# Sums of G go to DRAM through the buffer of the joined stage's first rows; the last pair's split and store written behind w_down's second products

## The chip, the cores and the metric

One core of one Trainium2 chip runs the whole kernel. The metric is the device time of one execution in microseconds (us), lower being better. Before the change the median of three runs is 1064.61 us (1063.67 to 1065.51).

The names of the engines are TensorE (PE in the profile; its weight loads are PEld), VectorE (DVE), ScalarE (ACT), GpSimd (POOL) and SyncE (SP). SP issues nearly all DMA transfers, in one queue and in order: an issue that waits holds up every issue behind it. GpSimd issues a few transfers of its own.

## The reference, cut to what matters

The kernel computes one decoder layer on 256 tokens of 2048 features, in float32: attention of two kinds, and then a gated feed-forward block. The change lies in the second half of that block.

```python
h = rmsnorm(x, pre_ffn_g[l])
u = causal_dwconv(h @ w_up[l], conv_w[l], conv_b[l])      # 2048 -> 2 x 5632
gate, val = jnp.split(u, 2, axis=-1)
y = (jax.nn.gelu(gate, approximate=True) * val) @ w_down[l]   # 5632 -> 2048
x = x + rmsnorm(y, post_ffn_g[l])
```

G below is gelu(gate) * val, transposed: its 5632 features lie in 44 blocks of 128, and each block holds 256 tokens.

## The kernel before, in words

**Precision.** Each float32 operand is split into a high and a low part. ScalarE casts the high part (`split`, or `w_split` for weights: the lines L120 and L321) and VectorE subtracts it for the low part (L123 and L322). TensorE then makes three products for one: high by high, high by low, low by high. The split weights lie in five rotating buffers (`wpair`), the raw weights in five others (`raw`), and SP refills a raw buffer when VectorE has read it.

**Stages around the change.** The 44 blocks are worked in two halves of 22, and a pair `g` is two blocks, so a half has 11 pairs. In the *gate stage* (about 340 to 578 us) TensorE makes the gate and the value of the pairs 0 to 10 from w_up (L301), ScalarE and VectorE make G of each pair from them. Then come the *w_down products* of the first half for the output columns 0 to 1023 (about 578 to 649 us, L1039). Then the *joined stage* (to about 940 us) makes the second half's gates and values, and between them the first half's products for the columns 1024 to 2047. At the end come the second half's w_down products.

**Seven products in place of eight.** Some pairs multiply a 2 by 2 block matrix of G by one of w_down with seven block products (`seven`). That needs four sums of G's blocks, which GpSimd makes for each pair (`sums_of_y`, L1148 to L1151), and sums of w_down's blocks. The latter are made either on the spot by four VectorE additions (`add`, L1052; pairs 0, 2 and 4 of the columns 0 to 1023), or ahead of time during the gate stage, kept in DRAM (`t_dram`, made by `stage`), and loaded when they are due (pairs 1, 3 and 5). A pair whose sums come from `t_dram` loads them in two pieces: one into a `raw` buffer, the other, `two`, into a buffer of its own with the tag gb0. The other pairs of that part (`four`) are multiplied the plain way.

**Order of the w_down products for the columns 0 to 1023.** The loop runs over i = 0 to 4. At i = 0 it does the first part of pair 0's seven products (banks a, b, e), then 24 plain products, then pair 0's other four (d, f, c, g), and then all seven of pair 1. At i = 1 it does the same with the pairs 2 and 3, at i = 2 with the pairs 4 and 5. Each product of a bank is three matmuls. So TensorE comes to pair 1's t1 and t3 (banks d, f), then to t2 and t4 out of `two` (banks c, g), and then to pair 2.

**Where G's sums go.** The sums of the pairs 0 to 5 stay on the chip. Those of the pairs 6 to 10 are needed only in the joined stage. They are split into a tile `late` of 128 by 1024 (512 KB) with the tag gb0, and GpSimd stores that in DRAM (`s_dram`, L1321 to L1325), from where `late_sums` fetches it when it is due. A tag without a count is one buffer. So `late` of five pairs, then `two` of the pairs 1, 3 and 5, and then the joined stage's rows named `low` take turns in gb0, each waiting for the one before it to be used up. The buffer gb2 holds nothing until the joined stage's first rows, named `top` (512 KB), are loaded into it.

**What orders the work.** TensorE's order is the code's. The other engines' order is set by a scheduler up to the joined stage, which starts an instruction early when its buffers are free; from the joined stage on the order of ScalarE, VectorE and SP is the code's. So an instruction can stand in an engine's queue far from where the code has it.

Of the kernel before, what the change touches and what calls it, by code (L numbers as in the profile page):

```python
# [9 lines left out]
F32R = mybir.dt.float32r  # L10
# [7 lines left out]
P = 128  # L18
# [7 lines left out]
FHALF = 22  # L26
# [9 lines left out]
def hybrid_layer(ctx: ExitStack, tc: tile.TileContext, x, pre_mix_g, w_in, b_forget, sinks,  # L36
# [3 lines left out]
    pe, act, dve, pool, sp = nc.tensor, nc.scalar, nc.vector, nc.gpsimd, nc.sync  # L40
# [13 lines left out]
    def bank(tag="acc"):  # L54
        return ps.tile([P, 512], F32, tag=tag, bufs=4, name="bank_" + tag)
# [13 lines left out]
    UNIT = 1024  # L69
# [250 lines left out]
    def split(hi, lo, src):  # L320
        act.copy(hi, src)  # L321
        dve.tensor_tensor(lo, src, hi.bitcast(F32), op=ALU.subtract)  # L322
# [531 lines left out]
    with tc.tile_pool(name="ffn", bufs=1) as fp:  # L854
# [30 lines left out]
        def rows_of(b):  # L885
            u = ubuf[cnt[0] % NU]
            cnt[0] += 1
            if type(b) is list:
                for m, x in enumerate(b):
                    c = fp.tile([P, 256], F32, tag="cs", bufs=1, name="cs")  # L890
                    act.copy(c, x[:, 256:512])
                    dve.tensor_tensor(u[:, m, 2:258], x[:, 0:256], c, op=ALU.add)
                    pool.tensor_tensor(u[:, m, 2:258], u[:, m, 2:258], rowf, op=ALU.mult)
            else:
                dve.tensor_tensor(u[:, :, 2:258], b.rearrange("p (m c) -> p m c", m=2),  # L895
                                  both(rowf, 256), op=ALU.mult)
            return [u[:, m, :] for m in range(2)]
# [111 lines left out]
        kept_sums = {}  # L1009
# [116 lines left out]
        def gated(us, c0, yy):  # L1126
            gates = []
            for m, u in enumerate(us):
                gates.append(conv(u, c0 // P + m, yy[:, m, :]))
            return gates  # L1130
# [11 lines left out]
        def sums_of_y(half, g, ys):  # L1142
            s = fp.tile([P, 512], F32, tag="s", name="s")
            (a11, a21), (a12, a22) = [(y[:, 0:P], y[:, P:256]) for y in ys]
            s2, s3, s4, s1 = (s[:, i * P:i * P + P] for i in range(4))
            if g < least[half]:
                s1 = a21
            pool.tensor_tensor(s3, a11, a21, op=ALU.subtract)  # L1148
            pool.tensor_tensor(s1, a21, a22, op=ALU.subtract)
            pool.tensor_tensor(s2, s1, a11, op=ALU.subtract)  # L1150
            pool.tensor_tensor(s4, a12, s2, op=ALU.add)  # L1151
            return s
# [5 lines left out]
        def split_sums(half, g, s):  # L1158
            w, *parts = sums_at(half, g)
            split(*parts, s[:, :w])  # L1160

        def joined():

            steps = FHALF // 2
# [58 lines left out]
            for g in range(steps + 1):  # L1223
# [14 lines left out]
                if g:  # L1238
                    if g <= most[1]:
                        s = sums_of_y(1, g - 1, ys)  # L1240
# [49 lines left out]
        for half in range(2):  # L1290
            if half:
                with tc.manual_schedule(engines={mybir.EngineType.Activation, mybir.EngineType.DVE,
                                                 mybir.EngineType.SP}):
                    joined()
            for g in range(0 if half else FHALF // 2):
                c0 = g * 256
                alt = g % 2
                if g == 0:
                    bg = first_gate()
                    order.__exit__(None, None, None)  # L1300
                    bv = [bank(), bank()]
                    proj_T(w_up, DFF + c0, bv, LONG)
                else:
                    bg = bank("att") if alt else bank()
                    proj_S(w_up, c0, bg, LATE if g == 1 else LONG)
                yy = fp.tile([P, 4, 256], F32, tag="yy", bufs=2, name="yy")
                gates = gated(rows_of(bg), c0, yy)
                gelu(gates)
                if g:
                    bv = bank("att") if alt else bank()  # L1310
                    proj_S(w_up, DFF + c0, bv, LONG)
                ys = valued(rows_of(bv), c0, yy, gates)
                if g == 0:
                    for t in range(2):
                        sp.dma_start(x_dram[t * P:(t + 1) * P, :], x_sb[:, t, :])
                s = sums_of_y(0, g, ys)
                for m, y in enumerate(ys):
                    split_G(0, g, m, y)
                if g < most[0]:
                    split_sums(0, g, s)  # L1320
                else:  # L1321
                    x = fp.tile([P, UNIT], F32R, tag="gb0", name="late")
                    split(x[:, 0:512], x[:, 512:1024], s)
                    kept_sums[g] = tc.dram_tile([P, UNIT], F32R, name="s_dram")
                    pool.dma_start(kept_sums[g], x)  # L1325
                if not g:
                    four_of = main.tile([P, 4, 4, 256], F32, tag="y", name="staged")
                    rooms = [four_of[:, i] for i in range(4)]
                    start = 0
                    for at in STORED:  # L1330
                        start = stage(*at, start, 7,
                                      lambda: rooms.append(rooms[0]) or rooms.pop(0))
            if half == 1:
                rest = main.tile([P, KT, 512], F32R, tag="hT", name="rest")
                whole, halves = slice(0, 512), [slice(0, 256), slice(256, 512)]

            assert not todo
            if not half:
                y_sb = main.tile([P, 2, D], F32, tag="y", name="y_sb")
            for n in (0, 2) if half else (0,):  # L1340
                opened = []
                tail = half and n
                at = SEVENS[half][n // 2]
                shared = [bank("att") for _ in range(4 if at else 0)]
                b, e, g = [bank() for _ in range(3)]
                h = None if tail else bank()
                for i in range(FHALF // 2 - len(at)):
                    here = [u for u, x in enumerate(at) if x == i]
                    begun = [lambda u=u: seven(half, n, u, u == len(at) - 1, (b, e, g, *shared), opened)
                             for u in here]  # L1350
                    others = begun[0]() if begun else None
                    four(half, n, len(at) + i, (b, g), opened)
                    if not tail:
                        four(half, n + 1, len(at) + i, (e, h), opened)
                    if others:
                        others()
                    for x in begun[1:]:
                        x()()
                    if at and i == at[-1]:
                        fold(half, n, *shared)  # L1360
                    if i == max((0, *at)):
                        if gains:
                            past = small.tile([P, 1], F32, tag="ry", bufs=2, name="past")
                            tc.keep_in_program_order(
                                pool.tensor_scalar(past, y_sb[:, 1, 1536:1537], 1.0, None,
                                                   op0=ALU.mult))
                        for args, kw in gains:
                            tc.keep_in_program_order(pool.tensor_tensor(*args, **kw))
                    if tail and i == (at[-1] + 4 if at else 0):
                        b1 = [bank("att"), bank("att")]  # L1370
                        for x, cs in zip(b1, halves):
                            pe.matmul(x[:, cs], G[1][0][:, 0:P], G[1][0][:, 0:256], start=True,
                                      stop=False)
                            act.copy(x[:, cs], y_sb[:, 1, 1536:2048][:, cs])
                if half and not tail:
                    gbf = [fp.tile([P, UNIT], F32, tag=f"gb{i}", name=f"gbc_ffn{i}")
                           for i in range(2)]
                    for i, x in enumerate(gbf):
                        cs = slice(i * UNIT, (i + 1) * UNIT)
                        sp.dma_start(x, post_ffn_g[0, cs].partition_broadcast(P))  # L1380
                later_on = None if tail else lambda *args, **kw: gains.append((args, kw))
                for t, x in enumerate((b, g)):
                    down(half, t, n, x, later_on)
                if not tail:
                    for t, x in enumerate((e, h)):
                        down(half, t, n + 1, x, later_on)
# [45 lines left out]
        for t in range(2):  # L1432
            i = sp.dma_start(x_sb[:, t, :], x_dram[t * P:(t + 1) * P, :])
# [58 lines left out]
```

## Time and profile before

| what | value |
|---|---|
| median of three runs | 1064.61 us (1063.67 to 1065.51) |
| the profiled execution, its own time | 1066.2 us |
| its span, first to last instruction | 1064.5 us |
| TensorE busy | 1043.9 us, 98% |
| VectorE busy | 860.3 us, 81% |
| ScalarE busy | 631.7 us, 59% |
| GpSimd busy | 197.8 us, 19% |
| mean granted TensorE clock | 0.992 |
| DRAM traffic | 223 GB/s over the span |

The profile is of one execution. Times in its rows count from the start of the span. A row of the timeline has the start and the length of a group of like instructions, the engine, the line of the code, the operation, what it writes and reads, and the count; in square brackets stands how long the engine had been idle before it, and what it had waited for. A row of the chain of waits has the start, the length and the instruction that held up the end. Rows of stretches give each engine's busy time within a stretch of time, and PEclk, the share of the full clock that TensorE was granted in it. The DMA share is that of 16 engines, and it can go a little over 1.

### The profile page before, as it was taken

How to read it: one execution, taken by the hardware profiler on the slowest of the kernel's cores; microseconds unless marked ns; L12 is line 12 of the kernel's file. 1: busy time of each engine (PE TensorE's matmuls, PEld its weight loads, DVE VectorE, ACT ScalarE, POOL GpSimd, SP SyncE). 2: the span in 40 equal slices, each digit the busy share in tenths (PEclk: the TensorE clock that was granted, in tenths of full speed). 3: DMA queues.
4: the chain of work that ended last, by engine and by line, in shares of the span. 5: the costliest groups of instructions: out<-in, count | busy, mean ns of one | idle time of the engine just before them, and what ended most of it. 6: DMA issues, size and time to landing. Idle time of an engine off the chain costs nothing.

```text
span 1064.5 us, 19057 instructions
## 1 busy us (share of the span) xinstructions
PE 1043.9 (98%) x7225; PEld 958.9 (90%) x7225; DVE 860.3 (81%) x1372; ACT 631.7 (59%) x1041; POOL 197.8 (19%) x244
## 2 busy tenths in 40 slices
PE   9999999999999999999999699999999999999996
PEld 7899988888888999999999489999999999988886
DVE  5999877887468889988888587888888888799793
ACT  6777657667557556546565364555555555656561
POOL 3253255441122311111111200111110000000023
PEclk9999999999999999999999799999999999999999
DMA  8645657555875889999975686666666666767783
GB/s 279 202 128 170 182 158 221 168 169 160 298 235 197 266 265 335 298 317 309 301 240 178 197 248 212 197 199 197 198 199 213 211 214 209 252 196 249 267 311 114
DMA packets 184232, 238.46 MB, mean 224 GB/s; under 512 B 8236, under 2 KB 153036, under 8 KB 183244
## 3 DMA queue, kind: packets, MB, share of 16 engines
q1 hardware_dynamic: 180780, 231.54, 67.6%
q0 software_dynamic: 3040, 5.24, 1.7%
q8 instruction: 56, 0.92, 0.3%
q10 hardware_dynamic: 320, 0.47, 0.1%
q14 instruction: 36, 0.29, 0.1%
HBM read 220.82 MB, written 16.27 MB: 223 GB/s over the span
## 4 chain that ended last, share of the span: by engine, by line
PE 86%; DVE 5%; DMA 3%; ACT 2%; POOL 2%; issue 2%; SPq 0%; DVEq 0%; ACTq 0%; POOLq 0%
PE bank_acc L301 31%; PE bank_acc L1039 13%; PE bank_acc L318 12%; PE bank_att L301 11%; PE bank_att L1039 6%; PE bank_acc L264 5%; PE bank_acc L271 3%; DVE wpair L123 2%; PE bank_att L318 1%; POOL scr L451 1%; PE bank_att L519 1%; DMA raw<-in_w_in_dram 1%; PE bank_att L484 1%; PE bank_att L528 1%; DMA low<-in_w_down_dram 1%
## 5 line engine op out<-in xcount | busy, mean ns | idle before, releaser
L123 DVE TENSOR_TENSOR wpair<-raw,wpair 128x1024 fp32r<-128x1024 f32 (+3 forms) x311 | 372.1, 1221 | 58.9 <-ACT wpair L120 57.8
L120 ACT CAST wpair<-raw 128x1024 fp32r<-128x1024 f32 (+3 forms) x310 | 312.9, 1030 | 125.7 <-PE bank_acc L301 51.5
L301 PEld LDWEIGHTS bank_acc<-hT,wpair 128*128 128x128 f32 x2976 | 341.3, 188 | 1.8
L301 PE MATMUL bank_acc<-hT,wpair 128*128 128x256 f32 x2976 | 342.1, 276 | 0.0
L1039 PE MATMUL bank_acc<-wpair,G 128*128 128x512 f32 x546 | 136.1, 392 | 0.3 <-DVE wpair L322 0.2
L1039 PEld LDWEIGHTS bank_acc<-wpair,G 128*128 128x128 f32 x546 | 102.9, 189 | 22.6 <-DVE wpair L322 0.6
L301 PE MATMUL bank_att<-hT,wpair 128*128 128x256 f32 x1056 | 120.7, 276 | 0.0
L301 PEld LDWEIGHTS bank_att<-hT,wpair 128*128 128x128 f32 x1056 | 120.2, 188 | 0.1
L264 PE MATMUL bank_acc<-hT,wpair 128*128 128x512 f32 x384 | 94.9, 394 | 0.0
L264 PEld LDWEIGHTS bank_acc<-hT,wpair 128*128 128x128 f32 x384 | 69.5, 188 | 13.2
L318 PE MATMUL bank_acc<-wpair,oT 128*128 128x512 f32 x336 | 78.0, 391 | 0.0
L318 PEld LDWEIGHTS bank_acc<-wpair,oT 128*128 128x128 f32 x336 | 62.6, 188 | 12.8
L1148 POOL TENSOR_TENSOR s<-yy 128x128 f32<-128x128 f32 x16 | 13.7, 853 | 309.3 <-DVE yy L1139 309.3
L900 ACT ACTIVATE yy<-u,cw 128x256 f32<-128x256 f32 x88 | 48.3, 594 | 31.7 <-DVE u L895 28.4
L321 ACT CAST wpair<-low 128x1024 fp32r<-128x1024 f32 x32 | 33.7, 1053 | 35.3 <-PE bank_acc L301 14.0
L895 DVE TENSOR_TENSOR u<-bank_acc,rowf 128x512 f32<-128x512 f32 x31 | 21.3, 689 | 38.5 <-PE bank_acc L301 38.5
L321 ACT CAST G<-yy 128x256 fp32r<-128x256 f32 x44 | 16.3, 405 | 58.8 <-DVE yy L1139 36.5
L271 PE MATMUL bank_acc<-hT,wpair 128*128 128x256 f32 x384 | 49.5, 280 | 0.0
L271 PEld LDWEIGHTS bank_acc<-hT,wpair 128*128 128x128 f32 x384 | 47.4, 188 | 1.4
L318 PE MATMUL bank_acc<-wpair,hT 128*128 128x384 f32 (+1 forms) x288 | 47.7, 321 | 0.0
L321 ACT CAST wpair<-raw 128x1024 fp32r<-128x1024 f32 (+1 forms) x39 | 34.4, 896 | 19.6 <-PE bank_acc L1039 6.6
L318 PEld LDWEIGHTS bank_acc<-wpair,hT 128*128 128x128 f32 x288 | 45.4, 188 | 0.1
(270 smaller groups left out, 1378.2 us busy)
## 6 DMA issues: line engine op xcount, KB each, us to landing
raw<-in_w_up_dram SPq DMA_DIRECT2D x176, 512.0 KB, 5.2
raw<-in_w_down_dram SPq DMA_DIRECT2D x53, 512.0 KB, 4.8
raw<-in_w_in_dram SPq DMA_DIRECT2D x51, 512.0 KB, 5.5
raw<-in_w_out_dram SPq DMA_DIRECT2D x32, 512.0 KB, 4.2
staged<-in_w_down_dram SPq DMA_DIRECT2D x36, 256.0 KB, 6.4
t_dram<-staged SPq DMA_DIRECT2D x18, 512.0 KB, 6.6
low<-in_w_down_dram SPq DMA_DIRECT2D x16, 512.0 KB, 4.6
raw<-t_dram SPq DMA_DIRECT2D x13, 512.0 KB, 5.7
```

Of the source, the lines that this page charges most:

```text
L120: i1 = act.copy(hi[:, cs], raw[:, cs])
L123: i2 = dve.tensor_tensor(lo[:, cs], raw[:, cs], hi[:, cs].bitcast(F32), op=ALU.subtract)
L264: pe.matmul(b, hi[:, a, m * P:(m + 1) * P], hT[:, kt, 0:512], start=(kt == 0), stop=(last == (0, kt)))
L271: pe.matmul(b[:, 256:512], lo[:, a, m * P:(m + 1) * P], hT[:, u * 4 + a, 0:256], start=False, stop=(last == (1, u * 4 + a)))
L301: pe.matmul(b[:, m * 256:(m + 1) * 256], ws[:, a, m * P:(m + 1) * P], hT[:, kt, i * 256:(i + 1) * 256], start=not begun, stop=last == (low ...
L318: pe.matmul(b, a, r[:, cols], start=(first and i == 0), stop=(last and i == 2))
L321: act.copy(hi, src)
L451: pool.tensor_tensor(dst, dst, row, op=ALU.mult)
L895: dve.tensor_tensor(u[:, :, 2:258], b.rearrange("p (m c) -> p m c", m=2), both(rowf, 256), op=ALU.mult)
L900: act.activation(y, u[:, 2:258], AF.Identity, bias=cw[:, 3, ch:ch + 1], scale=cw[:, 2, ch:ch + 1])
L1039: pe.matmul(b, x, r, start=b not in opened and not i, stop=closes and i == 2)
L1148: pool.tensor_tensor(s3, a11, a21, op=ALU.subtract)
```

## The change

The split and the store of a pair's sums become a function, `keep_sums`, whose tile `late` has the tag gb2 in place of gb0. The pairs 6 to 9 call it where they did before. The last pair, 10, calls it later in the code: in the loop over the w_down products, at i = 1, behind the products of the pairs 2 and 3.

```diff
+        def keep_sums(g, s):
+            x = fp.tile([P, UNIT], F32R, tag="gb2", name="late")
+            split(x[:, 0:512], x[:, 512:1024], s)
+            kept_sums[g] = tc.dram_tile([P, UNIT], F32R, name="s_dram")
+            pool.dma_start(kept_sums[g], x)
...
                 if g < most[0]:
                     split_sums(0, g, s)
-                else:
-                    x = fp.tile([P, UNIT], F32R, tag="gb0", name="late")
-                    split(x[:, 0:512], x[:, 512:1024], s)
-                    kept_sums[g] = tc.dram_tile([P, UNIT], F32R, name="s_dram")
-                    pool.dma_start(kept_sums[g], x)
+                elif g < FHALF // 2 - 1:
+                    keep_sums(g, s)
...
                     for x in begun[1:]:
                         x()()
+                    if not half and i == 1:
+                        keep_sums(FHALF // 2 - 1, s)
```

No instruction is added or taken away. TensorE, ScalarE and GpSimd have their instructions in the same order as before; on ScalarE and VectorE the last pair's split still stands ahead of the split of pair 1's t1 and t3 (the row `wpair<-raw` before `wpair<-two`), although the code now has it behind. SP's queue and a few rows of VectorE are what moves.

The first place is SP's queue in the gate stage, at about 400 us. Here `staged` and `t_dram` belong to the sums of w_down that are made ahead, and each row has in brackets the semaphores that it waits for: DMAHW those of earlier transfers of SP, DMASW of GpSimd's, the others of engines. Before:

```order
L75 DMA raw<-in_w_up_dram 128x4x256 [waits DMAHW0_49,DVE_49]
L923 DMA staged<-in_w_down_dram 128x2x256 [waits DMAHW1_49]
L923 DMA staged<-in_w_down_dram 128x2x256 [waits DMAHW2_49]
L75 DMA raw<-in_w_up_dram 128x4x256 [waits DMAHW3_49,DVE_49]
L932 DMA t_dram<-staged 512x1x256 [waits DMAHW4_49]
```

And the same place now:

```order
L75 DMA raw<-in_w_up_dram 128x4x256 [waits DMAHW7_49,DVE_49]
L923 DMA staged<-in_w_down_dram 128x2x256 [waits DMAHW0_49]
L923 DMA staged<-in_w_down_dram 128x2x256 [waits DMAHW1_49]
L75 DMA two<-t_dram 128x1024 [waits DMAHW5_49,DMAHW2_49]
L75 DMA raw<-in_w_up_dram 128x4x256 [waits DMAHW3_49,DVE_49]
L932 DMA t_dram<-staged 512x1x256 [waits DMAHW4_49]
```

The load of pair 1's `two` has come here from a place about 190 us later, and waits for the store of its two halves. In exchange a row has gone from SP's queue at the start of the gate stage: the load of the first `top`, issued there at 338.8 us before.

The second place is SP's queue at the w_down products of the pairs 1 to 3, at about 590 to 608 us. Before:

```order
L75 DMA raw<-in_w_down_dram 128x512 [waits DMAHW5_49,DVE_49]
L75 DMA raw<-in_w_down_dram 128x1024 [waits DMAHW7_49,DVE_49]
L75 DMA two<-t_dram 128x1024 [waits DMASW3_49,DMASW2_49,DMASW5_49,DMASW1_49,DMASW0_49]
L75 DMA two<-t_dram 128x1024 [waits DMAHW7_49,DMAHW0_49,DVE_49]
L75 DMA raw<-t_dram 128x1024 [waits DMAHW1_49,DVE_49]
```

And now:

```order
L75 DMA raw<-in_w_down_dram 128x512 [waits DMAHW5_49,DVE_49]
L75 DMA raw<-in_w_down_dram 128x1024 [waits DMAHW7_49,DVE_49]
L75 DMA two<-t_dram 128x1024 [waits DVE_49]
L75 DMA top<-in_w_down_dram 128x1024 [waits DMASW3_49,DMASW5_49,DMASW2_49,DMAHW0_49,DMASW1_49,DMASW0_49]
L75 DMA raw<-t_dram 128x1024 [waits DMAHW1_49,DVE_49]
```

The first of the two rows `two` was pair 1's, and waited for GpSimd's stores of `late`; the one that is left is pair 3's, and waits for VectorE to have read pair 1's. The wait for GpSimd's stores now stands on `top`, one row later, ahead of pair 3's `raw<-t_dram`.

The third place is VectorE at the pairs 1 and 2, from the low part of pair 1's `two` on. The rows L1052 are pair 2's additions, `low` is its second load, and the two rows L123 are the plain products' weights of i = 1. This is a piece of the difference, with - for before and + for now:

```order
 L322 TENSOR_TENSOR wpair<-two,wpair 128x1024
 L322 TENSOR_TENSOR wpair<-raw,wpair 128x512
-L322 TENSOR_TENSOR wpair<-low,wpair 128x1024
 L1052 TENSOR_TENSOR raw<-raw 128x512
-L123 TENSOR_TENSOR wpair<-raw,wpair 128x1024
+L322 TENSOR_TENSOR wpair<-low,wpair 128x1024
 L1052 TENSOR_TENSOR raw<-raw,low 128x512
 L123 TENSOR_TENSOR wpair<-raw,wpair 128x1024
 L1052 TENSOR_TENSOR low<-low,raw 128x512
-L322 TENSOR_TENSOR wpair<-raw,wpair 128x1024
-L1052 TENSOR_TENSOR low<-low 128x512
+L123 TENSOR_TENSOR wpair<-raw,wpair 128x1024
+L1052 TENSOR_TENSOR low<-low 128x512
+L322 TENSOR_TENSOR wpair<-raw,wpair 128x1024
```

Each of the additions has moved one place forward, and so `low` stands behind one addition, and the first of the plain weights behind two. The same piece comes once more, at the pairs 3 and 4.

## The prediction

> **What bounds the kernel now.** I read the page first, of an execution with a span of 1064.5 us. Its row of engines and its row of granted clock say:
>
> ```profile
> PE 1043.9 (98%) x7225; PEld 958.9 (90%) x7225; DVE 860.3 (81%) x1372; ACT 631.7 (59%) x1041; POOL 197.8 (19%) x244
> ...
> PEclk9999999999999999999999799999999999999999
> ```
>
> TensorE is busy for 98% of the span, so only its idle time and its slow time can be won without changing its work. The one slice in which its clock falls short is the 23rd of 40, at about 585 to 612 us. The second view is that of who waited for whom, TensorE alone:
>
> ```profile
> PE bank_att L1039 <- ACT wpair L321: 8.4, 2, 7.6
> ```
>
> It heads that list: 8.4 us in two waits, the longest 7.6, in the w_down products (L1039), for ScalarE's cast of weights. The third view is the chain of waits between 555 and 660 us, which tells what held up that cast:
>
> ```profile
> 591.38 5.41 DMA s_dram<-late
> ...
> 596.87 3.66 DMA two<-t_dram
> ```
>
> To be read downwards: the last pair's split is stored in DRAM (5.41 us); only then is gb0 free, and pair 1's `two` is loaded into it (3.66 us); the cast comes behind. Both transfers lie bare on the path. The fourth view is TensorE's timeline:
>
> ```profile
> 580.14 5.60 PE L1039 MATMUL bank_acc<-wpair,G 128*128 128x512 f32 x24
> 585.58 0.84 PE L1039 MATMUL bank_att<-wpair,G 128*128 128x512 f32 x3
> ...
> 591.35 0.50 PE L1039 MATMUL bank_att<-wpair,G 128*128 128x512 f32 x1 [0.84 <-ACT wpair L321]
> 592.61 0.73 PE L1039 MATMUL bank_att<-wpair,G 128*128 128x512 f32 x2 [0.76 <-DVE wpair L322]
> 593.18 0.99 PE L1039 MATMUL bank_att<-wpair,sums 128*128 128x512 f32 x3
> 601.72 0.79 PE L1039 MATMUL bank_att<-wpair,sums 128*128 128x512 f32 x1 [7.56 <-ACT wpair L321]
> 602.98 1.22 PE L1039 MATMUL bank_att<-wpair,sums 128*128 128x512 f32 x2 [0.47 <-DVE wpair L322]
> 604.00 1.48 PE L1039 MATMUL bank_acc<-wpair,G 128*128 128x512 f32 x3
> 605.28 1.48 PE L1039 MATMUL bank_att<-wpair,G 128*128 128x512 f32 x3
> ...
> 608.34 5.60 PE L1039 MATMUL bank_acc<-wpair,G 128*128 128x512 f32 x24
> ```
>
> From 580.14 to 585.58 it starts 24 matmuls in 5.44 us, 0.227 us each: full pace. From 604.00 to 605.28 three take 1.28 us, 0.427 each: half pace. The stretches of the fifth view say why:
>
> ```profile
> 590.30:593.70 3.40, 1.80 (x7) 1.05 (x6) 1.92 (x2) 0.99 (x2) 0.74 (x2) 1.00 0.84 214
> 593.70:594.20 0.50, 0.47 (x2) 0.00 (x0) 0.00 (x0) 0.00 (x0) 0.00 (x0) 0.54 1.12 301
> 594.20:601.70 7.50, 0.00 (x0) 0.00 (x0) 0.00 (x0) 1.07 (x2) 0.00 (x0) 0.50 0.60 215
> 601.70:607.30 5.60, 5.11 (x11) 3.73 (x12) 5.60 (x7) 3.52 (x5) 0.00 (x0) 0.50 0.30 97
> 607.40:613.00 5.60, 5.60 (x26) 4.63 (x25) 4.41 (x6) 3.17 (x4) 0.12 (x1) 1.00 0.75 232
> ```
>
> The third number from the end is the granted clock: full until 593.7, half until about 607.35, then full. It fell before the long wait, while TensorE still worked, right after the two short gaps at 590.5 and 591.8.
>
> **The stall goes.** Pair 1's `two` is now loaded at about 404 us, ahead of its use by some 190 us. The cast of `two` then follows ScalarE's cast before it. ScalarE's rows:
>
> ```profile
> 589.73 0.62 ACT L321 CAST late<-s 128x512 fp32r<-128x512 f32 x1 [3.83 <-POOL s L1151]
> 590.25 1.04 ACT L321 CAST wpair<-raw 128x1024 fp32r<-128x1024 f32 x1
> 600.63 1.04 ACT L321 CAST wpair<-two 128x1024 fp32r<-128x1024 f32 x1 [9.33 <-DMA two<-t_dram]
> 601.58 0.61 ACT L321 CAST wpair<-raw 128x512 fp32r<-128x512 f32 x1
> ```
>
> Casts of that size follow each other at 0.95 us (600.63 to 601.58), so `two` is cast from 591.20 to 592.24. The weight buffer that it needs is that of pair 0's t1 and t3, last read before TensorE turned to pair 1, ahead of the row of 591.35. Pair 1's f starts at 593.18 and its three matmuls are issued by 593.86. Behind them stand c and g of pair 1 and a, b and e of pair 2: 15 matmuls, 3.40 us at full pace. The 24 plain products could start at 597.26 in place of 608.34. **That is 11.08 us**: 7.86 us of standing still (593.86 to 601.72), and 3.22 us by which 601.72 to 608.34 is longer than 3.40, from half pace and the 0.47 us wait.
>
> **What is late next.** VectorE. Its rows after the stall:
>
> ```profile
> 591.33 1.23 DVE L322 TENSOR_TENSOR wpair<-raw,wpair 128x1024 fp32r<-128x1024 f32 x1 [0.25 <-ACT wpair L321]
> 601.70 1.23 DVE L322 TENSOR_TENSOR wpair<-two,wpair 128x1024 fp32r<-128x1024 f32 x1 [9.15 <-ACT wpair L321]
> 602.85 0.69 DVE L322 TENSOR_TENSOR wpair<-raw,wpair 128x512 fp32r<-128x512 f32 x1
> 603.45 1.22 DVE L322 TENSOR_TENSOR wpair<-low,wpair 128x1024 fp32r<-128x1024 f32 x1
> 604.58 0.69 DVE L1052 TENSOR_TENSOR raw<-raw 128x512 f32<-128x512 f32 x1
> 605.18 1.22 DVE L123 TENSOR_TENSOR wpair<-raw,wpair 128x1024 fp32r<-128x1024 f32 x1
> ```
>
> A large one takes a place of 1.15 us, a small one or an addition 0.60. The row of 591.33 stays, since the last pair's split is still ahead of it; so `two` comes at 592.48, the small one at 593.63, the addition at 594.23, `low` at 594.83, the second addition at 595.96, and the first plain weights (L123) at 596.56, done by 597.79. The two additions that the new order puts ahead cost the plain weights one more place, 0.60 us. The second plain matmul, the first that needs the low part, would start at 597.49: 0.30 us late. Later steps have room: the second plain weights come two places on, at about 599.5, and are needed 2.7 us after the first. At full clock the gain is 11.08 - 0.30 = **10.78 us**.
>
> **The clock, which the trace doesn't show for the changed kernel.** The two short gaps stay, for ScalarE still waits for GpSimd's sums until 589.7. If the clock falls after them as it did, TensorE goes on at half pace from 593.7. One end: it doesn't fall, cost nothing. The other: half pace lasts as long as it did once work had begun again, 601.72 to 607.35, 5.6 us; at 0.427 us that is 13 matmuls where 25 fit, 12 late by 0.227, 2.7 us. There is no reason for a gain. I take the middle, 1.34 us, since the long stretch of before had 7.86 us of idleness ahead of it and a further wait within. This delay covers the 0.30 us of VectorE. **The sum: 11.08 - 1.34 = 9.74 us.** By the Trainium skill (TensorE: Matmul & The Clock Gate, Part 1: The HAM clock gate), full clock comes back after about 3.4 us of sustained work; as an estimate from that page half pace would then cost 1.6 us and the gain be 9.5 us.
>
> **Edits at nothing, and their cover.** Moving the first `top` from 338.8 to about 597 us: its first cast is at 636.4.
>
> ```profile
> L321 ACT CAST wpair<-top x1: 624/624/624, 636.4 to 636.4; 128x512 fp32r<-128x512 f32 x1
> ```
>
> The five stores of `late` took this long from issue to landing:
>
> ```profile
> DMA to landing us min/median/max: 3.3/3.4/5.4
> ```
>
> And loads of the same size from `t_dram`, in the median of 13:
>
> ```profile
> raw<-t_dram SPq DMA_DIRECT2D x13, 512.0 KB, 5.7
> ```
>
> On SP `top` now waits for the last store, due by 596.8, and pair 3's `raw<-t_dram` and all later loads queue behind it. That one waits for the L123 above anyway, 597.8, so the wait is covered by 1.0 us; landing at 603.5, cast and subtracted it is ready by 605.8. TensorE needs it 45 matmuls (10.2 us) after 597.26, at 607.5 or later. If that cover of 1.7 us went, each us more would cost one. Pair 3's `two` goes out at 593.7, nine us earlier than now, and has longer still. The stores of the pairs 6 to 9 change their buffer only. The shift holds to the end: behind 607 us TensorE's waits come to this one of 0.2 us.
>
> ```profile
> PE bank_acc L1039 <- DVE wpair L322: 0.2, 1, 0.2
> ```
>
> The stretch where `two` is put now:
>
> ```profile
> 400.00:412.00 12.00, 12.00 (x108) 12.00 (x107) 11.90 (x22) 6.85 (x9) 1.07 (x2) 1.00 1.03 341
> ```
>
> TensorE is busy throughout, while the DMA engines are full (share 1.03). At 341 GB/s 512 KB take 1.5 us, which the weights loaded ahead should hide: from nothing to 1.5 us, taken as nothing.
>
> **How the numbers follow.** The profiled execution took 1066.2 us, 1.6 more than the median, so the same step would put its like at 1056.5; I take the gain from the median: 1064.61 - 9.74 = 1054.9 us. A measurement of this kernel can tell about 0.2%, 2.1 us, from no change.
>
> - **Forecast**, 1054.9 us: 0.52.
> - **The clock stays full**: the gaps of 0.84 and 0.76 us alone don't bring it down in most executions. For it: what follows them now is work, not idleness. Against it: the 0.54 in the row of 593.7. 1064.61 - 10.78 = 1053.8 us: 0.28. The same page (HAM oscillation) asks for a gap over about 3.4 us before the clock falls, which gives this time; the row of 593.7 doesn't agree.
> - **A new wait at pair 3**, for `raw<-t_dram` behind `top`, or for VectorE: a load of 5.7 us taking twice that costs 5.7 - 1.7, less what half pace hides, about 3.4 us. Against it: the DMA share of 0.30 there. 1058.3 us: 0.08.
> - **The early load hurts the gate stage**, 1.5 us: 1056.4 us: 0.07.
> - **Nothing comes of it**: the wait at 594 is ended by something else just as late. The order of ScalarE, where the written move of the last split changed nothing, shows how that could be; but no other partner of `two` is late. 1064.6 us: 0.03.
> - **Slower**: GpSimd's last store starves beside loads that now go on, and holds SP behind `top`. It starts to cost when it lands after 600.8 (pair 3 needed at 608.8, less 5.7, 1.05 and 1.23) and costs one for one; over 12 us of that, a landing after 612.6, is slower than before by 2.1 us. Five stores took 3.3 to 5.4; this would need 21. At 24 us it gives 1069.5 us: 0.02.
>
> The range goes from the full clock less what the runs of before spread downward (1064.61 - 1063.67 = 0.9), 1052.9, to the new wait at pair 3, 1058.3. Faster: all but the last two, 0.95; same 0.03; slower 0.02.
>
> **What would show it.** Right: the wait of 7.6 us is gone; the cast of `two` starts near 591.2; the plain products of i = 1 start between 597.5 and 599.9; the two short gaps are still there; pair 3 waits for nothing. The granted clock behind 593 tells forecast and first rival apart. Wrong: a wait over 2 us at the pairs 2 or 3, any gap between 400 and 560, or an SP row `top` issued well behind 597.

## The result and the profile after

| | before | after |
|---|---|---|
| median, same chip, in turns | 1065.06 us (1063.67 to 1066.15, 4 runs) | 1054.6 us (1053.86 to 1055.45, 4 runs) |
| the profiled execution, its own time | 1066.2 us | 1055.45 us |
| its span | 1064.5 us | 1053.7 us |
| mean granted TensorE clock | 0.992 | 0.997 |

The ratio is 0.9903, with a 95% interval of 0.9886 to 0.992: about 1% faster. The forecast was 1054.9 us. One execution of the experiments below, the profiled one of `low` behind pair 3's loads, took 1746.65 us at a granted clock of 0.556 and stands in none of the times.

The page's rows of engines and of granted clock, after:

```profile
PE 1041.1 (99%) x7225; PEld 957.0 (91%) x7225; DVE 861.3 (82%) x1372; ACT 631.7 (60%) x1041; POOL 199.3 (19%) x244
...
PEclk9999999999999999999999999999999999999999
```

The digit 7 at the 23rd slice is gone. Who waited for whom, TensorE alone, between 555 and 660 us after (the columns are the total, the count and the longest wait):

```profile
PE bank_att L1039 <- ACT wpair L321: 1.4, 1, 1.4
PE bank_att L1039 <- DVE wpair L322: 0.8, 1, 0.8
```

The wait of 7.6 us is gone, and what is left are the two short gaps ahead of pair 1. ScalarE's timeline after:

```profile
589.19 0.62 ACT L321 CAST late<-s 128x512 fp32r<-128x512 f32 x1 [3.83 <-POOL s L1151]
589.71 1.04 ACT L321 CAST wpair<-raw 128x1024 fp32r<-128x1024 f32 x1
590.66 1.04 ACT L321 CAST wpair<-two 128x1024 fp32r<-128x1024 f32 x1
591.61 0.61 ACT L321 CAST wpair<-raw 128x512 fp32r<-128x512 f32 x1
```

`two` is cast right behind the cast before it, with no idle time in front: the row of before had 9.33 us of it. The first row is the cast of the last pair's sums: ScalarE still waits 3.83 us for GpSimd there, as before, and pair 1's casts come behind it. TensorE's timeline after, with the same matmuls as the rows of before:

```profile
588.60 0.84 PE L1039 MATMUL bank_acc<-wpair,sums 128*128 128x512 f32 x3
590.80 0.51 PE L1039 MATMUL bank_att<-wpair,G 128*128 128x512 f32 x1 [1.36 <-ACT wpair L321]
592.06 0.73 PE L1039 MATMUL bank_att<-wpair,G 128*128 128x512 f32 x2 [0.75 <-DVE wpair L322]
592.64 2.33 PE L1039 MATMUL bank_att<-wpair,sums 128*128 128x512 f32 x6
594.76 1.48 PE L1039 MATMUL bank_acc<-wpair,G 128*128 128x512 f32 x3
596.04 1.09 PE L1039 MATMUL bank_att<-wpair,G 128*128 128x512 f32 x3
596.97 0.85 PE L1039 MATMUL bank_acc<-wpair,G 128*128 128x512 f32 x3
597.65 0.84 PE L1039 MATMUL bank_acc<-wpair,sums 128*128 128x512 f32 x3
598.33 5.60 PE L1039 MATMUL bank_acc<-wpair,G 128*128 128x512 f32 x24
```

From f (592.64) to the 24 plain products (598.33) it takes 5.69 us; before it was 593.18 to 608.34, 15.16 us. So the step itself gives 9.47 us. The three matmuls at 594.76 take 1.28 us up to the next row, which is half pace, and those at 596.97 take 0.68, full pace. The stretches after say the same of the granted clock (third number from the end):

```profile
590.30:593.10 2.80, 1.54 (x6) 1.05 (x7) 2.54 (x4) 2.80 (x5) 0.55 (x1) 1.00 1.00 237
593.20:596.50 3.30, 3.30 (x10) 2.52 (x9) 3.27 (x5) 2.04 (x3) 0.00 (x0) 0.50 1.05 331
596.60:602.00 5.40, 5.40 (x26) 4.45 (x25) 5.34 (x6) 2.98 (x4) 0.00 (x0) 1.00 0.81 278
```

The clock fell after the two gaps, as before, but for 3.4 us (593.14 to 596.55) where before it was 13.65 (593.74 to 607.39). SP's queue after:

```profile
593.17 0.33 SPq L75 DMA_DIRECT2D two<-t_dram  x1
596.65 0.33 SPq L75 DMA_DIRECT2D top<-in_w_down_dram  x1
597.38 0.33 SPq L75 DMA_DIRECT2D raw<-t_dram  x1
```

`top` waits for the last store, and pair 3's `raw<-t_dram` goes out behind it at 597.38 and lands at 603.90. TensorE doesn't wait for it.

### The profile page after: what moved, and what is told of

It reads as the page before. It is cut to its first block, busy times and chain, and to the rows that moved or that the text cites. A ratio compares the mean times of both kernels' runs of the same rounds, so it can differ in the third digit from the quotient of the medians.

```text
span 1053.7 us, 19053 instructions
## 1 busy us (share of the span) xinstructions
PE 1041.1 (99%) x7225; PEld 957.0 (91%) x7225; DVE 861.3 (82%) x1372; ACT 631.7 (60%) x1041; POOL 199.3 (19%) x244
## 4 chain that ended last, share of the span: by engine, by line
PE 84%; DVE 6%; DMA 3%; ACT 2%; issue 2%; POOL 2%; SPq 0%; DVEq 0%; ACTq 0%; POOLq 0%
PE bank_acc L301 31%; PE bank_acc L1039 12%; PE bank_acc L318 12%; PE bank_att L301 10%; PE bank_att L1039 6%; PE bank_acc L264 5%; PE bank_acc L271 3%; DVE wpair L123 2%; PE bank_att L318 1%; DMA low<-in_w_down_dram 1%; POOL scr L451 1%; PE bank_att L519 1%; DMA raw<-in_w_in_dram 1%; PE bank_att L484 1%; PE bank_att L528 1%
## 5 line engine op out<-in xcount | busy, mean ns | idle before, releaser
L123 DVE TENSOR_TENSOR wpair<-raw,wpair 128x1024 fp32r<-128x1024 f32 (+3 forms) x311 | 372.2, 1222 | 58.5 <-ACT wpair L120 57.6
L1039 PE MATMUL bank_acc<-wpair,G 128*128 128x512 f32 x546 | 135.4, 391 | 0.1
L1039 PEld LDWEIGHTS bank_acc<-wpair,G 128*128 128x128 f32 x546 | 102.5, 189 | 21.9 <-DVE wpair L123 0.5
L322 DVE TENSOR_TENSOR wpair<-raw,wpair 128x1024 fp32r<-128x1024 f32 (+1 forms) x39 | 39.6, 1029 | 7.5 <-ACT wpair L321 7.1
```

The source lines that it names most:

```text
L123: i2 = dve.tensor_tensor(lo[:, cs], raw[:, cs], hi[:, cs].bitcast(F32), op=ALU.subtract)
L1039: pe.matmul(b, x, r, start=b not in opened and not i, stop=closes and i == 2)
```

## The experiments

All times are medians on the same chip as a run of the kernel before; each ratio is to that, whose median was 1065.27, 1066.08 and 1066.3 us on the three chips. The theory is that of the prediction: what was won is the row of store, load and cast through gb0, and what is left are two short gaps and a clock that falls after them. The first rival is that the new place of the split in the code does it, and the second question what the two gaps and the clock are worth. Where the expectations use letters, A is the prediction's account, the rivals have the letters behind it, and F is the theory that the place alone led to.

**The buffer alone.** The kernel before with one tag changed; the split and the store stay where the code had them.

```diff
-                    x = fp.tile([P, UNIT], F32R, tag="gb0", name="late")
+                    x = fp.tile([P, UNIT], F32R, tag="gb2", name="late")
```

> One half of the change alone: the sums of all five pairs pass through gb2, and the last pair's split and store stay where the code had them before. Theory A, the buffer does it all and the written place nothing, since the scheduler puts the split back where it was: the time of the changed kernel, 1054.6 us within its spread of about 1 us, with the two short gaps of TensorE at pair 1 and its cast of `two` right behind the cast before it. Rival B, the later place in the code gives a part of the gain: over 1056.5 us, and a wait at pair 1 of over 2 us.

Measured: 1055.7 us (1054.4 to 1059.24), ratio 0.991 (0.9892 to 0.9929). The order of the instructions on every engine is that of the changed kernel. So in this change the buffer makes the gain, and the new place in the code makes nothing, since the scheduler sets the split back ahead of pair 1. The two times differ by 1.1 us, less than the spread of this run. Its profiled execution is its slowest; there the half clock lasted 6.83 us:

```profile
593.30:599.90 6.60, 6.04 (x14) 4.78 (x15) 6.57 (x9) 4.55 (x6) 0.00 (x0) 0.50 1.05 324
```

**The place alone.** The changed kernel with the old buffer. With gb0 the last pair's tile can only come behind pair 3's `two`, so here the split really is late.

```diff
-            x = fp.tile([P, UNIT], F32R, tag="gb2", name="late")
+            x = fp.tile([P, UNIT], F32R, tag="gb0", name="late")
```

> The other half alone: the last pair's split and store stand behind the products of the pairs 2 and 3 in the code, and pass through gb0 as before. Now gb0 is taken by pair 1's and pair 3's `two` first, and the split can't be put back; pair 5's `two` waits for the last store. Theory A says that what costs is a `two` that waits for a store, wherever it stands: pair 1 waits for nothing and the two short gaps go as well (about 2.1 us, and 1.6 us of half pace in those executions where the clock fell), and at pair 5 a wait may come: the last `two` of pair 3 is read at about 603, so the split ends at 606, the store lands at 609.5 to 611.7, `two` at 613 to 618.5, ready 2.3 us later, 615.5 to 621, and TensorE wants it at about 620.6. So 1051.0 to 1052.5 us, at worst 1 us more. Rival B, the place gives only a part and the buffer is needed for the rest: 1056 to 1060 us, with a wait of several us at pair 5.

Measured: 1056.37 us (1056.17 to 1057.13), ratio 0.9912 (0.9899 to 0.9926). That missed, and lies in the range of rival B, but without the wait of several us at pair 5 that it goes by. The stall is gone here too, so the place takes it away as the buffer does, once the split can't be put back. The first half of the expectation came true: no gaps of 1.36 and 0.75 us, a clock that stays full, and at 597 us a lead of 4.0 us over the changed kernel. But it was given back. GpSimd's timeline in this kernel, the four sums of the last pair:

```profile
585.38 5.78 POOL L1148 TENSOR_TENSOR s<-yy 128x128 f32<-128x128 f32 x1 [20.65 <-DVE yy L1139]
591.13 0.90 POOL L1149 TENSOR_TENSOR s<-yy 128x128 f32<-128x128 f32 x1
592.11 1.32 POOL L1150 TENSOR_TENSOR s<-s,yy 128x128 f32<-128x128 f32 x1
593.51 0.79 POOL L1151 TENSOR_TENSOR s<-yy,s 128x128 f32<-128x128 f32 x1
```

In the changed kernel the first of them takes 2.91 us and the other three 0.45 or 0.46 each. VectorE beside them, whose instructions of these sizes take 0.69 and 1.22 us elsewhere:

```profile
590.16 0.68 DVE L322 TENSOR_TENSOR wpair<-raw,wpair 128x512 fp32r<-128x512 f32 x1
590.88 0.83 DVE L1052 TENSOR_TENSOR raw<-raw 128x512 f32<-128x512 f32 x1
591.63 1.48 DVE L322 TENSOR_TENSOR wpair<-low,wpair 128x1024 fp32r<-128x1024 f32 x1
593.04 0.94 DVE L1052 TENSOR_TENSOR raw<-raw,low 128x512 f32<-128x512 f32 x1
```

While GpSimd's first sum runs, and up to the first of these rows, each VectorE instruction starts some 0.08 us before the one ahead of it ends. The first pause is that from 590.84 to 590.88, and GpSimd's first sum ends at 591.16, 0.32 us after its start. The additions and the low parts behind it are the slow ones. And SP, where pair 4's `low` waits for GpSimd to have read the buffer that it shares with `yy`:

```profile
594.32 0.33 SPq L75 DMA_DIRECT2D low<-in_w_down_dram  x1
...
596.51 0.55 SPq L75 DMA_DIRECT2D raw<-t_dram  x1
```

In the changed kernel `low` goes out at 589.18. Here it and what is behind it go out with pair 3's load, which takes 8.4 us to land (604.90). TensorE then waits at pair 3:

```profile
607.36 0.72 PE L1039 MATMUL bank_att<-wpair,G 128*128 128x512 f32 x2 [0.76 <-DVE wpair L322]
...
613.30 5.07 PE L1039 MATMUL bank_acc<-wpair,G 128*128 128x512 f32 x21 [0.68 <-DVE wpair L123]
```

The lead is 2.6 us at 604.7, 1.4 behind the first of these, 0.2 at the second, and at 946 us the kernel is 0.7 behind. From this came a further theory: GpSimd's first sum doesn't come to its end while VectorE runs without a pause, and what is queued behind it (the late split, `low` on SP) gives the gain back.

**The split behind pair 1's.** The changed kernel, buffer gb2, with the split of the last pair tied behind the cast and subtraction of `two`.

```diff
-            split(x[:, 0:512], x[:, 512:1024], s)
+            parts = split(x[:, 0:512], x[:, 512:1024], s)
+            if pair1:
+                for i, first in zip(parts, pair1):
+                    tc.add_manual_dep(
...
```

> The changed kernel, with the last pair's split tied behind the split of pair 1's `two` on ScalarE and VectorE, so that it really stands later. Theory A: the two short gaps (1.4 and 0.8 us) go, and with them the fall of the clock: no granted clock under 1.00 between 20 and 1040 us in the profile, and 2.1 us plus 1.6 us (in about half of the executions) less than the changed kernel: 1051.0 to 1052.5 us. Rival D, the gaps only cover a wait for VectorE, which has the same work to do before the plain products: a wait of 1.5 us or more at pair 2 or at the plain products, and 1053.5 us or more.

Measured: 1057.8 us (1054.87 to 1059.82, 6 runs), ratio 0.9923 (0.9906 to 0.9939). That missed too: the time is rival D's, though no single wait reaches the 1.5 us that it names. GpSimd is late again. Its first sum, and VectorE's rows around its end (line numbers are shifted by up to 3):

```profile
586.11 5.18 POOL L1151 TENSOR_TENSOR s<-yy 128x128 f32<-128x128 f32 x1 [20.54 <-DVE yy L1142]
```

```profile
589.76 1.21 DVE L321 TENSOR_TENSOR wpair<-two,wpair 128x1024 fp32r<-128x1024 f32 x1
593.99 0.69 DVE L321 TENSOR_TENSOR wpair<-raw,wpair 128x512 fp32r<-128x512 f32 x1 [3.02 <-ACT wpair L321]
```

The sum ends at 591.29, 0.32 us after VectorE fell idle at 590.97. ScalarE stood before the late split for 4.19 us meanwhile, and held the casts behind it; the last store went out at 595.83 and landed at 605.26. `top` waits for that store, and the loads behind it on SP go out late:

```profile
605.35 0.33 SPq L75 DMA_DIRECT2D top<-in_w_down_dram  x1
```

```profile
610.66 0.62 ACT L321 CAST wpair<-raw 128x512 fp32r<-128x512 f32 x1 [2.84 <-DMA raw<-in_w_down_dram]
```

TensorE is 0.2 us ahead of the changed kernel at 611 us and 2.3 behind at 614, which is nearly all that it loses. Here the clock stayed full without a gain. In the changed kernel the two engines show the same thing, earlier:

```profile
584.74 2.91 POOL L1148 TENSOR_TENSOR s<-yy 128x128 f32<-128x128 f32 x1 [19.45 <-DVE yy L1139]
```

```profile
586.11 1.23 DVE L322 TENSOR_TENSOR wpair<-raw,wpair 128x1024 fp32r<-128x1024 f32 x1
589.84 0.69 DVE L322 TENSOR_TENSOR late<-s,late 128x512 fp32r<-128x512 f32 x1 [2.50 <-ACT late L321]
```

VectorE falls idle at 587.34 and the sum ends at 587.65, 0.31 later. The same time from VectorE's first pause to the end of the sum is 0.31 to 0.33 us in all nine traces in which GpSimd makes this sum. No run takes VectorE's work away, so that it is what holds the sum rests on these times.

The Trainium skill (SBUF — State Buffer, Who interferes with whom) has a rule for this: a VectorE instruction with two inputs in SBUF contends with a GpSimd instruction that reads SBUF, over a port that one of them holds at a time. The sums that end 0.3 us after the start of VectorE's first pause agree with it.

**The last pair alone.** The kernel before, with gb2 for the last pair only.

```diff
-                    x = fp.tile([P, UNIT], F32R, tag="gb0", name="late")
+                    x = fp.tile([P, UNIT], F32R, name="late",
+                                tag="gb2" if g == FHALF // 2 - 1 else "gb0")
```

> Only the last pair's sums pass through gb2, the other four through gb0 as before, all at the old place in the code. Pair 1's `two` then waits for the store of the pair before the last, landed at 569, and is loaded at about 569 to 577 in place of 403. Theory A, only the last store was in the way and it doesn't matter how early `two` comes: the changed kernel's time, 1054.6 us, at most 1 us more, since `low` of pair 0 is issued behind that load. Rival C, the load had to leave the w_down stage altogether, whose transfers are in each other's way: pair 0 or 1 waits over 1.5 us more, 1056.5 us or more.

Measured: 1056.62 us (1056.11 to 1057.03), ratio 0.9913 (0.99 to 0.9927), within the spread of the buffer alone. By the expectation this is rival C's number, just over its 1056.5 us. But the wait that rival C names isn't there: `two` is loaded from 568.80 to 572.63, and the gap ahead of pair 1 is 1.98 us, as in the profile of the buffer alone, where `two` comes at 403. So for the stall to go it is enough that the last pair's store doesn't stand before `two`; whether the early load is worth a further us the intervals leave open. The clock fell for 3.4 us.

**The sums on VectorE.** The changed kernel, in which VectorE makes the last pair's four sums.

```diff
-            pool.tensor_tensor(s3, a11, a21, op=ALU.subtract)
+            q = dve if not half and g == FHALF // 2 - 1 else pool
+            q.tensor_tensor(s3, a11, a21, op=ALU.subtract)
...
```

> The changed kernel, with the last pair's four sums made by VectorE in place of GpSimd. Theory F, formed after the first runs: TensorE's two short gaps come from GpSimd, whose first sum takes 2.9 us where 0.5 is its usual time, until VectorE pauses; and where the gaps were taken away by other means (the split tied behind, or put behind pair 3) VectorE didn't pause, the sum took 5.2 and 5.8 us, and SP's load of `low` for pair 4, which waits for that sum, held up pair 3's loads. If the sums cost VectorE four short operations of about 0.25 us and nothing waits for GpSimd, the plain products start near 594.6 in place of 598.3, the clock doesn't fall, and the time is 1051.0 to 1053.0 us. Rival D, VectorE is the next bound and gives all of it back: 1053.5 us or more, with waits for VectorE of over 2 us at the pairs 1 to 3.

Measured: 1053.89 us (1052.78 to 1056.05), ratio 0.9884 (0.9869 to 0.99). That is 0.9 us over the range of theory F and in rival D's, though no wait for VectorE comes near its 2 us. TensorE's row of the plain products and the cast of pair 3's load on ScalarE:

```profile
594.51 5.60 PE L1039 MATMUL bank_acc<-wpair,G 128*128 128x512 f32 x24
```

```profile
603.71 1.05 ACT L321 CAST wpair<-raw 128x1024 fp32r<-128x1024 f32 x1 [2.60 <-DMA raw<-t_dram]
```

Both gaps go and the clock stays full: the plain products start 3.82 us earlier than in the changed kernel, as forecast (594.6). But now TensorE is early enough to wait for pair 3's load (0.77 us at 606), and 1.44 us of the lead is left at 946. So the wait for GpSimd's sums is what made the two gaps.

**The gaps filled.** The changed kernel with ten matmuls of no use into bank b, six ahead of pair 1's d and four behind its first matmul. They change bank b's sum, and with it pair 1's part of the output; the expectation is wrong in that they take no part.

```diff
+                    fill(b, 6)
+                    pe.matmul(d, s1[0], t1[0], start=False, stop=False)
+                    fill(b, 4)
```

> The changed kernel, with ten matmuls of zeros added into bank b where TensorE stands still at pair 1: six before the first of t1's products and four between it and the next (0.22 us each). They take no part in the result. If the two gaps are what brings the clock down, there is no stretch under 1.00 between 20 and 1040 us, the 15 matmuls ahead of the plain products take 3.4 to 3.7 us in place of 5.0, and the median is 1053.4 to 1054.2 us with a spread under 1 us. Rival: the clock falls for another reason, or the added matmuls come in the way: 1054.6 us or more, with half pace in some runs.

Measured: 1054.44 us (1054.29 to 1055.37), ratio 0.9889 (0.9874 to 0.9904). The profile has no idle time at pair 1 and a full clock throughout:

```profile
592.99 1.53 PE L1039 MATMUL bank_att<-wpair,sums 128*128 128x512 f32 x6
...
597.28 3.07 PE L1039 MATMUL bank_acc<-wpair,G 128*128 128x512 f32 x11
```

From f to the plain products it takes 4.29 us, against 5.69 with the clock's fall. The 15 matmuls ahead of the plain products take 3.60 us, as expected; the median is 0.2 us over the expected range and 0.2 under the rival's. The time is too near the changed kernel's to show the 1.4 us by itself. Nor does one profile show that the filling kept the clock up, as the next run tells.

**The changed kernel again**, on the chip of the last two.

> The changed kernel once more, as the measure for the other three on the same chip: 1054.6 us, between 1053.8 and 1055.5; those executions in which the clock fell some 1.3 us longer than the others.

Measured: 1054.98 us (1054.43 to 1057.48), ratio 0.9897 (0.9882 to 0.9912); one execution lies 2 us over the expected range. In its profile the same two gaps stand (1.25 and 0.76 us), and the clock did not fall:

```profile
593.20:596.50 3.30, 3.30 (x16) 2.49 (x15) 3.27 (x6) 2.06 (x4) 0.00 (x0) 1.00 0.99 322
```

From f (592.82) to the plain products (597.12) it takes 4.30 us, as with the gaps filled. So the fall is not fixed by the order of the instructions: it came in four of the five profiles that have these gaps (before, after, the buffer alone, the last pair alone).

**`low` behind pair 3's loads.** The place alone, with pair 4's `low` set behind pair 3's loads on SP.

```diff
+                if not half and not n and u == 4:
+                    for first in pair3:
+                        tc.add_manual_dep(
+                            issued[-1].ins, first.ins.name,
...
```

> The place alone again (last pair's split behind pair 3, buffer gb0), with pair 4's `low` tied on SP behind pair 3's loads. Theory F: then the slow GpSimd sum holds up only `low`, which has time; pair 3's `raw<-t_dram` goes out before 596 and lands by 603, TensorE's wait for its cast at 606 to 607 goes, and the time is 1 to 2 us under that of the place alone: 1054.4 to 1055.4 us. Rival: the SP queue was not what came late, and VectorE's waits at the plain products remain: 1056 us or more.

Measured: 1052.88 us (1052.82 to 1054.2, 4 runs), ratio 0.9876 (0.986 to 0.9893), 1.5 us under the expected range. Its trace can't be read beside the others, and the kernel was run once more:

> This is the kernel in which the last pair's split has gb0 again, behind pair 3's `two`, and pair 4's `low` is issued by SyncE behind pair 3's loads, once more and with five rounds. The theory that SyncE held back pair 3's load: the time is about 1052.9 us again, under that of the changed kernel; in the trace pair 3's `raw<-t_dram` goes out before 595 us (596.5 with `low` ahead of it), TensorE has no wait over 0.3 us at 606 to 608, and the clock stays full. The theory that `low` only happened to stand there: pair 3 waits for 0.7 us at 607 as it did, and the time is 1054.5 to 1056.5 us.

Measured: 1052.56 us (1052.36 to 1053.07), ratio 0.9874 (0.9857 to 0.989). SP, TensorE's waits between 555 and 660 us, and TensorE's row of the plain products (L126 and L1042 are L123 and L1039 of the changed kernel):

```profile
595.91 0.33 SPq L77 DMA_DIRECT2D raw<-t_dram  x1
596.33 0.38 SPq L77 DMA_DIRECT2D low<-in_w_down_dram  x1
```

```profile
PE bank_acc L1042 <- DVE wpair L126: 0.6, 1, 0.6
```

```profile
595.94 5.50 PE L1042 MATMUL bank_acc<-wpair,G 128*128 128x512 f32 x23 [0.61 <-DVE wpair L126]
```

Pair 3's load goes out 0.6 us earlier than in the place alone, not 1.5 as expected, since it also waits for a VectorE that GpSimd slows (its L126 takes 1.48 us and ends at 595.88). The larger part is the landing: 4.57 us (at 600.48) where it took 8.39 (at 604.90). In the place alone `low`, three more loads and this one went out between 594.32 and 596.51; here the three had gone out ahead of `low`, the last of them, pair 3's `two`, at 590.76 in place of 595.98. TensorE waits for nothing at pair 3, and the clock stays full. The one wait left is 0.6 us, and the lead of 2.6 us over the changed kernel at the second plain product is still 2.4 at 946. This version has the lowest median: eight runs of 1052.36 to 1054.2 against eight of the changed kernel of 1053.86 to 1057.48, medians 1052.8 and 1054.9, not all on one chip; on the chip that ran both, it was 1052.88 against 1054.98.

**Both.** The same, with the last pair's sums on VectorE; the edit is that of the sums above.

> The kernel with `low` behind pair 3's loads, and the last pair's four sums made by VectorE. Theory that GpSimd's sums are slow and slow VectorE down while VectorE works without a pause: with them gone VectorE's casts of the low part keep 1.22 us (1.48 with GpSimd beside them), the plain products of i = 1 start by 594.6 us and pair 3 waits for nothing: 1051 to 1052.7 us. Rival, that the sums only change places: VectorE has four instructions of about 0.25 us more on its path just where it is the late one, so the time is that of the kernel beside it or up to 1 us more, 1052.9 to 1053.9 us.

Measured: 1053.61 us (1052.27 to 1054.8), ratio 0.9884 (0.9869 to 0.9898). The rival's number. The slow row of the low part is gone from VectorE, but its four instructions more, 0.81 us in all, are a part of what makes it late for pair 1:

```profile
590.99 0.74 PE L1042 MATMUL bank_acc<-wpair,G 128*128 128x512 f32 x2 [1.25 <-DVE wpair L325]
```

Whether it is slower than the kernel beside it the intervals leave open.

Not tried: a fourth buffer of its own for `late`; whether the memory has room for it isn't shown here.

## Why the prediction was right, point by point

- **The stall goes.** Right. The cast of `two` starts at 590.66 (591.20 forecast); ScalarE's cast before it starts 0.54 us earlier too (589.71 against 590.25), by which this execution was ahead.
- **VectorE late next by 0.30 us.** Right as a term that the clock covers, and a little larger: in the trace without the fall, f to the plain products takes 4.30 us, against 4.08 worked out for full clock (597.26 less 593.18), 0.22 more, and the second plain matmul, for which the term was worked out, starts 0.45 us late (597.57); with the fall it shows nowhere.
- **The clock.** The fall came as forecast and its size was a little under: from f to the plain products it took 5.69 us in place of 4.08, so 1.61 us, where the middle of two bounds was taken as 1.34. That middle had no mechanism behind it, and that it came near is luck. The reason given for less than the upper bound holds in this execution, in which half pace lasted 3.41 us and not 5.6. It is no rule: in the buffer alone, without the long idle stretch too, half pace lasted 6.83 us, and f to the plain products (594.88 to 601.39) took 2.43 us more than 4.08, near the upper bound of 2.7. The Trainium skill (TensorE: Matmul & The Clock Gate, Part 1: The HAM clock gate), from which the estimate of 1.6 us was worked out, says that full clock comes back after about 3.4 us of work, and this trace agrees.
- **The first rival**, that the clock stays full, is not wrong either. It is what another execution of the same kernel did. Of the four times of the result two, 1053.86 and 1054.02 us at a mean clock of 0.998, are near this rival's 1053.8, and two, 1055.17 and 1055.45 at 0.997, near the forecast's; only the last has a trace. The chances of 0.52 and 0.28 were put on something that changes from one execution to the next, and one profile of before could not give one number for it.
- **The sum.** 9.74 us forecast for the step, 9.47 in the trace. The spans differ by 10.8: 0.5 us is what lasted of a better start (the clock came up to full at 10.06 us in the profile of before and at 6.05 in that of after), 0.5 a smaller gap at 946, and 0.3 at the end. The gap of the medians is 10.5 us, with before's median 0.45 above the one that the forecast started from. So that the time came within 0.3 us of 1054.9 is luck in part: the gain was 0.7 us more than forecast, and before was 0.45 slower.
- **The edits at nothing** cost nothing. `top` went out at 596.65 and pair 3's load landed in 6.5 us; no wait at pair 3. The early `two` went out at 402.7 and landed in 6.9 us, the weights beside it took up to 9.8, and TensorE waited nowhere between 400 and 560 us. What the prediction did not see is how thin the cover at pair 3 is: the two versions that bring TensorE there 2.4 and 3.7 us earlier (the place alone, the sums on VectorE) wait there for 0.76 and 0.77 us, and the one in which the loads ahead of it go out early (`low` behind pair 3's loads) doesn't.
- **The order on ScalarE.** That the later place in the code moves nothing was read from the order, and the buffer alone shows it in time.

What fell is what was built on it afterwards: that a late last split would win the two gaps and the clock as well, 1051.0 to 1052.5 us. The gaps go and the clock stays full, but GpSimd's sum, VectorE and SP's queue gave it back.

## What to carry to other kernels

A buffer that two streams share orders them, and the queue that waits for it orders everything behind: here a DMA store, a DMA load and a cast in a row left the path when one tag changed. When a late piece of work is moved out of the way, follow what else waits for the engine that makes it; here a load that was due later (`low`) stood ahead in the same queue and held back one that was due sooner. And before counting any lead as won, see that the load that is due first stands first in an in-order queue.

## What the hardware showed

- The granted clock fell to half after gaps of 1.36 and 0.75 us close together, for 3.41 us; for 6.83 after 0.42, 1.98 and 0.77; and not at all after 1.25 and 0.76, all in executions of the same order of instructions. The Trainium skill (TensorE: Matmul & The Clock Gate, HAM oscillation) speaks of gaps over about 3.4 us; the row of 593.20 of the first profile of after, at 0.50, doesn't agree.
- The times between two changes of the granted clock are whole multiples of 3.413 us: half clock lasted 3.41, 6.83 or 13.65 us, and the full clock behind it 453.97 us (133 times 3.413) in each of the four traces with a fall. In the 3.41 us that end at the fall TensorE was busy for 1.81 us (before), 1.57 (after), 1.37 (the buffer alone) and 0.86 (the last pair alone). In the changed kernel again, counted back in the same steps from the change of clock at its end, the like piece had 1.97 us and no fall; 2.22 and 2.23 us (the split behind pair 1's, both) brought none either. So what parts these traces is the busy share of such a piece, 0.53 and less against 0.58 and more, and not a single gap. No run sets this share on purpose, so as a rule it isn't shown.
- A GpSimd sum of 128 by 128, whose like takes 0.45 us, took 2.91, 5.18 and 5.78 us while VectorE worked without a pause, and ended 0.31 to 0.33 us after VectorE's first pause began, even where that was one of 0.04 us. Where VectorE then went on, its instructions beside the further sums lengthened from 1.22 to 1.48 us.
- At a DMA share near 1 (400 to 412 us), transfers of 512 KB took 6.2 to 8.0 us to land before and up to 9.8 with one load more, without TensorE waiting. Pair 3's load took 8.39 us at a share of 0.96 (the place alone) and 4.57 at 0.86 (`low` behind pair 3's loads).
